# HGRN self scores by a GpSimd product and a ones matrix, with wider low-weight splits

## The chip, the cores and the metric

One core of a Trainium2 chip runs the whole program. The metric is device time in microseconds (us). Engine names follow the profile: PE is TensorE's matmul, PEld its weight load, DVE is VectorE, ACT is ScalarE, POOL is GpSimd, SP starts the DMAs.

## What is computed

A trunk of four layers over 256 tokens of 1024 features. Each layer is a half-weighted SwiGLU feed-forward block, a mixer, and a second feed-forward block, each on an RMS-normalised input and added to x. The mixers are HGRN2, neighbourhood attention, MLA, HGRN2; only the two HGRN2 layers are touched here. Cut to what matters, each of their 8 heads (128 features) does, in both directions of time:

```python
b = cumsum(logf within a chunk)
attn[t, s] = sum_d q[t, d] * exp(b[t, d] - b[s, d]) * k[s, d]      # s <= t forward, s >= t backward
o = attn @ v  (+ the state carried over from the other chunks)
```

For s = t the decay is one, so the score of a token with itself is the plain dot product of q with the sum of the forward key and the backward key, over 128 features.

## The kernel before, in words

**Layout.** Activations lie feature-major: 128 features on the partitions, 256 tokens along the row. Weights stream from HBM in slabs of 128x1024 floats, each holding eight 128x128 blocks. Products run in a split form: a weight or an activation in float32 is taken as a high part rounded to the fast format float32r and a low part, the remainder, and a product is three float32r matmuls (high by high, low by high, high by low: L352 to L354, or L399 to L401 where the activations are the stationary side).

**Slabs.** `fetch` allots a raw, a high and a low tile. `load_slab` (L330) issues the DMA, then `split` makes the high part on ACT in two copies of 512 columns (L326) and the low part on DVE by a subtraction (L327). With `long_split["on"]` the low part is one DVE instruction of 1024 columns; otherwise two of 512. The flag is on in the inner part of the feed-forward blocks (L622) and off in the mixers. `take` (L339) hands out blocks and keeps five slabs ahead.

**Order.** PE and SP run in the order in which the program is written. On ACT, DVE and POOL a planner in the framework orders the instructions by priority and by its own view of when they are ready. Every projection matmul group calls `step()`; every eighth step in HGRN calls `tick()`, which advances each pending task (a Python generator) by one `yield`, at a raised priority.

**HGRN.** `HG_ORDER` projects z and q of each head (zq0 to zq7), the gates (g0, g1) and the values (v0, v1). After each zq the generator `scores(h, ...)` is queued. Its first piece forms the decay f on ACT, the keys kq and the query q. Its second forms ks, the sum of both keys, on POOL (L723), and scales q by f on DVE (L743, L744). Then follow seven pieces for B = 1, 2, 4, ..., 64. Each piece makes four PE records of cross scores (L752), updates the queries and keys in place on DVE (L755, L757), copies the next keys on ACT (L727, the tile kc that the next piece's matmuls load), multiplies neighbouring decays on POOL (L761, tile T), and lays the scores into the tile A through a mask on DVE (L741). In the piece for B = 8 the self scores are also made: a float32 matmul of ks by q for each half of the tokens (L768), whose diagonal alone is kept by a masked copy. `outputs` then multiplies A by the values (L789) and normalises; `out_project` follows.

The tag "sq" has three buffers of 128x256; it serves squares, and the two halves `acc_r` of `row_norm`, which sums over the features by a matmul with the constant matrix of ones `ones_r` (L495).

Of the kernel before, what the change touches and what calls it, by code (L numbers as in the profile page):

```python
# [2 lines left out]
P = 128  # L3
T = 256
# [215 lines left out]
def emit(tc, i, o, plan):  # L220
# [5 lines left out]
    F32, F32R = mybir.dt.float32, mybir.dt.float32r  # L226
    I32, U8 = mybir.dt.int32, mybir.dt.uint8
    AF, ALU, AX = mybir.ActivationFunctionType, mybir.AluOpType, mybir.AxisListType
    nc = tc.nc
    V, A, G, TE = nc.vector, nc.scalar, nc.gpsimd, nc.tensor  # L230
    with ExitStack() as es:
# [10 lines left out]
        def bank(tag, shape, name):  # L242
            return pp.tile(shape, F32, tag=tag, name=name, bufs={"p": 4, "a": 3, "s": 1}[tag])

        def work(tag, shape, name, bufs=2, dt=F32):
            return wk.tile(shape, dt, tag=tag, name=name, bufs=bufs)

        def ap(t, off, dims):
            return bass.AP(tensor=t.tensor, offset=t.offset + off, ap=[list(t.ap[0])] + [list(d) for d in dims])

        def turns(t, n=T):

            return ap(t, 0, [[1, n // 2], [n // 2, 2]])

        def back(ps):

            return ap(ps, 0, [[1, 2], [2, T // 2]])

        def split2(t):
            return t.rearrange("p (a b) -> p a b", a=2)  # L260
# [6 lines left out]
        def tick():  # L267
            with tc.high_priority(URGENT):
                for g in list(tasks):
                    try:  # L270
                        next(g)
                    except StopIteration:
                        tasks.remove(g)
# [38 lines left out]
        long_split = {"on": False}  # L312
# [105 lines left out]
        ones_r = cp.tile([P, P], F32R, name="ones_r")  # L418
# [268 lines left out]
        def hgrn(s, idx, layer):  # L687
# [15 lines left out]
            def scores(h, pz, pq):  # L703
                while "R" not in nf:
                    yield
                R = nf["R"]
                z = work("w2", [P, 2, T], "z", 3)
                if len(pz) == 1:
                    V.tensor_tensor(z.rearrange("p e (a b) -> p e a b", a=2), ap(pz[0], 0, [[T, 2], [1, 2], [2, P]]), split2(R).unsqueeze(1).broadcast_to([P, 2, 2, P]), op=ALU.mult)
                else:  # L710
                    for e in range(2):
                        V.tensor_tensor(split2(z[:, e, :]), back(pz[e]), split2(R), op=ALU.mult)
                A.activation(z, z, AF.Tanh, scale=0.5)
                f = work("f", [P, 2, T], "f", 3)
                A.activation(f, z, AF.Identity, scale=c1[:, h:h + 1], bias=c0[:, h:h + 1])

                kq = work("kq", [P, 4, T], "kq", KQ_BUFS)
                A.activation(kq[:, 0::3, :], z, AF.Identity, scale=nc1[:, h:h + 1], bias=c1[:, h:h + 1])
                q = work("w1", [P, T], "q", 3)
                V.scalar_tensor_tensor(split2(q), back(pq), HG_SCALE, split2(R), op0=ALU.mult, op1=ALU.mult)  # L720
                yield
                ks = work("w1a", [P, T], "ks", 3)
                G.tensor_tensor(ks, kq[:, 0, :], kq[:, 3, :], op=ALU.add)  # L723

                def keys(B):
                    kc = work("kc", [P, T], "kc", 4)
                    A.copy(ap(kc, 0, [[2 * B, P // B], [B, 2], [1, B]]), ap(kq, 0, [[2 * B, P // B], [3 * T + B, 2], [1, B]]))  # L727
                    return kc

                def place(ps, B):  # L730
                    if B == 128:
                        A.copy(At[h][:, 1:3, :], ps)
                    elif B >= 32:
                        for a0 in range(0, P, 2 * B):
                            for sa, ta in ((a0, a0 + B), (a0 + B, a0)):
                                A.copy(At[h][sa:sa + B, 0::3, ta:ta + B], ps[sa:sa + B, :, ta:ta + B])
                    elif B == 1:
                        A.copy(At[h][:, 0::3, :], ps)
                    else:
                        m = 1 + MASK_LEVELS.index(B) if B else 0  # L740
                        V.copy_predicated(At[h][:, 0::3, :], msk[:, m:m + 1, :].broadcast_to([P, 2, P]), ps)  # L741

                V.tensor_tensor(kq[:, 2, :], q, f[:, 0, :], op=ALU.mult)  # L743
                V.tensor_tensor(kq[:, 1, :], q, f[:, 1, :], op=ALU.mult)  # L744
                kc = keys(1)
                yield
                Tt, nseg, B = f, T, 1
                while B <= 64:
                    pl = bank("a", [P, 2, P], f"A_{B}")
                    for t in range(2):  # L750
                        rhs = ap(kq, T + t * P, [[2 * B, 64 // B], [T + B, 2], [1, B]])
                        TE.matmul(pl[:, t, :], lhsT=kc[:, t * P:(t + 1) * P], rhs=rhs, start=True, stop=True)  # L752
                    n2 = nseg // 2
                    ev = ap(kq, 0, [[T, 2], [2 * B, n2], [1, B]])
                    V.tensor_tensor(ev, ev, ap(Tt, 1, [[nseg, 2], [2, n2], [0, B]]), op=ALU.mult)  # L755
                    od = ap(kq, 2 * T + B, [[T, 2], [2 * B, n2], [1, B]])
                    V.tensor_tensor(od, od, ap(Tt, 0, [[nseg, 2], [2, n2], [0, B]]), op=ALU.mult)  # L757
                    if B < 64:
                        kc = keys(2 * B)
                        Tn = work(f"T{B}", [P, 2, n2], f"T{B}", 3)  # L760
                        G.tensor_tensor(Tn, Tt[:, :, 0::2], Tt[:, :, 1::2], op=ALU.mult)  # L761
                        Tt = Tn
                    place(pl, B)
                    if B == 8:
                        pl = bank("s", [P, 2, P], "A_0")
                        for t in range(2):
                            c = slice(t * P, (t + 1) * P)
                            TE.matmul(pl[:, t, :], lhsT=ks[:, c], rhs=q[:, c], start=True, stop=True)  # L768
                        place(pl, 0)
                    nseg = n2  # L770
                    B *= 2
                    yield
                pl = bank("a", [P, 2, P], "A_128")
                TE.matmul(pl[:, 0, :], lhsT=kq[:, 3, P:], rhs=kq[:, 1, :P], start=True, stop=True)
                TE.matmul(pl[:, 1, :], lhsT=kq[:, 0, :P], rhs=kq[:, 2, P:], start=True, stop=True)
                place(pl, 128)
                scoring.discard(h)
# [43 lines left out]
            for kind in HG_ORDER:  # L821
                n = int(kind[-1])
                if kind[0] == "z":
                    if n:
                        pz = [bank("p", [P, 2, T], "z")]
                        project(pz[0][:, 0, :], xs)
                        project(pz[0][:, 1, :], xs)
                    else:
                        pz = [bank("p", [P, T], "z") for _ in range(2)]
                        beside(pz, xs)  # L830
                    pq = bank("p", [P, T], "q")
                    project(pq, xs)
                    while len(tasks) > HG_DEPTH:
                        tick()
                    scoring.add(n)
                    tasks.append(scores(n, pz, pq))
                    continue
                ps = [bank("p", [P, 512], kind) for _ in range(2)]
                natural(ps, xs, 512)
                if "h" not in nf:  # L840
                    nf["h"] = work("rh", [P, 2], "rh", 1)
                    V.tensor_scalar(nf["h"], nf["c"], 0.5, None, op0=ALU.mult)
                for t in range(2):
                    if kind[0] == "v":
                        A.activation(vt[t][n], ps[t], AF.Copy, scale=nf["c"][:, t:t + 1])
                    else:
                        half = nf["h"][:, t:t + 1]
                        gs = work("w2", [P, 512], "gs", 3)
                        A.activation(gs, ps[t], AF.Tanh, scale=half)
                        V.scalar_tensor_tensor(gt[t][n], gs, 1.0, ps[t], op0=ALU.add, op1=ALU.mult)  # L850
                if kind[0] == "g":
                    gated.append(n)
                if kind[0] == "v":
                    tasks.append(outputs(n))
            beat["every"] = 0
            tick()
            later(HG_LAST_1, tick)
            later(HG_LAST_2, tick)
# [442 lines left out]
```

## Time and profile before

| | |
|---|---|
| median of 3 runs (lowest to highest) | 1994.96 us (1994.09 to 1995.13) |
| the profiled execution's own time | 1996.11 us |
| its span, first to last instruction | 1993.8 us |
| PE busy, share of the span | 1974.6 us, 99% |
| DVE / ACT / POOL busy | 1690.8 / 1322.7 / 205.4 us |

The span is 2.3 us shorter than the profiled execution's own time, and that execution is 1.15 us slower than the median. Busy shares are averages over stages; the two HGRN stages run from about 182 to 332 us and from about 1645 to 1797 us of the span. The matmul ends in the profile are modelled: one 256-column matmul shows as 275 ns, but they overlap, so a run of them is read by the spacing of the starts, or from the chain of waits, which counts no time twice.

### The profile page before, as it was taken

How to read it: one execution, taken by the hardware profiler on the slowest of the kernel's cores; microseconds unless marked ns; L12 is line 12 of the kernel's file. 1: busy time of each engine (PE TensorE's matmuls, PEld its weight loads, DVE VectorE, ACT ScalarE, POOL GpSimd, SP SyncE). 2: the span in 40 equal slices, each digit the busy share in tenths (PEclk: the TensorE clock that was granted, in tenths of full speed). 3: DMA queues.
4: the chain of work that ended last, by engine and by line, in shares of the span. 5: the costliest groups of instructions: out<-in, count | busy, mean ns of one | idle time of the engine just before them, and what ended most of it. 6: DMA issues, size and time to landing. Idle time of an engine off the chain costs nothing.

```text
span 1993.8 us, 36877 instructions
## 1 busy us (share of the span) xinstructions
PE 1974.6 (99%) x13304; PEld 1838.4 (92%) x13304; DVE 1690.8 (85%) x3342; ACT 1322.7 (66%) x2988; POOL 205.4 (10%) x366
## 2 busy tenths in 40 slices
PE   9999999999999999999999999999999999999999
PEld 8999999999999998999999998899999999999998
DVE  8988998988888779988788879898888879989885
ACT  7665777666666578666566657676666657776663
POOL 1001320100000044100000022010000002411000
PEclk9999999999999999999999999999999999999999
DMA  6766434666666654566566653266656664445654
GB/s 229 241 203 204 149 129 136 198 209 201 199 202 202 204 203 152 170 203 203 197 201 200 202 192 128 92 196 208 201 195 204 203 210 157 141 137 177 205 169 159
DMA packets 103286, 369.34 MB, mean 185 GB/s; under 512 B 11456, under 2 KB 13248, under 8 KB 103104
## 3 DMA queue, kind: packets, MB, share of 16 engines
q1 hardware_dynamic: 103104, 366.99, 56.4%
q8 instruction: 105, 1.72, 0.4%
q14 instruction: 77, 0.63, 0.1%
HBM read 365.89 MB, written 1.05 MB: 184 GB/s over the span
## 4 chain that ended last, share of the span: by engine, by line
PE 89%; DVE 6%; ACT 2%; DMA 1%; issue 1%; POOL 0%; SPq 0%; DVEq 0%; ACTq 0%; POOLq 0%
PE gu L372 29%; PE gu L370 15%; PE dn L372 14%; PE dn L370 7%; PE A L752 2%; DVE wl L327 2%; PE out L352 1%; PE v L399 1%; PE out L354 1%; PE out L353 1%; PE v L401 1%; PE v L400 1%; PE z L352 1%; PE z L353 1%; PE z L354 1%; PE dn L354 1%
## 5 line engine op out<-in xcount | busy, mean ns | idle before, releaser
L327 DVE TENSOR_TENSOR wl<-raw,wh 128x512 fp32r<-128x512 f32 (+2 forms) x1077 | 890.8, 847 | 198.8 <-ACT wh L326 193.2
L326 ACT CAST wh<-raw 128x512 fp32r<-128x512 f32 (+1 forms) x1373 | 797.4, 617 | 362.1 <-issue 166.9
L372 PE MATMUL gu<-xw,wh 128*128 128x512 f32 x2816 | 893.6, 382 | 2.7 <-DVE xw L1249 2.5
L370 PE MATMUL gu<-xw,wl 128*128 128x256 f32 x2816 | 691.7, 273 | 0.7 <-DVE wl L327 0.7
L372 PEld LDWEIGHTS gu<-xw,wh 128*128 128x128 f32 x2816 | 504.5, 190 | 57.1 <-DVE xw L1249 3.1
L370 PEld LDWEIGHTS gu<-xw,wl 128*128 128x128 f32 x2816 | 531.2, 191 | 21.5 <-DVE wl L327 1.3
L372 PE MATMUL dn<-h,wh 128*128 128x512 f32 x1232 | 401.6, 382 | 0.0
L370 PE MATMUL dn<-h,wl 128*128 128x256 f32 x1232 | 326.9, 273 | 0.0
L372 PEld LDWEIGHTS dn<-h,wh 128*128 128x128 f32 x1232 | 229.4, 189 | 29.4
L370 PEld LDWEIGHTS dn<-h,wl 128*128 128x128 f32 x1232 | 236.2, 192 | 3.1 <-DVE wl L327 0.2
L608 ACT COPY gu<-gu 128x256 f32<-128x256 f32 x352 | 128.1, 370 | 123.5 <-PE gu L372 122.8
L609 DVE TENSOR_TENSOR gu<-gu 128x256 f32<-128x256 f32 x352 | 140.2, 417 | 5.3 <-ACT gu L608 5.3
L452 POOL TENSOR_TENSOR acc<-sq 128x256 f32<-128x256 f32 x13 | 10.6, 812 | 1121.4 <-ACT sq L449 1121.4
L399 PE MATMUL v<-wh,xw 128*128 128x256 f32 (+1 forms) x256 | 80.0, 313 | 0.0
L600 DVE SCALAR_TENSOR_TENSOR th<-th,gu 128x512 f32<-128x512 f32 (+1 forms) x96 | 61.7, 644 | 18.8 <-ACT th L599 18.8
L401 PE MATMUL v<-wh,xw 128*128 128x256 f32 (+1 forms) x256 | 77.1, 301 | 0.0
L400 PE MATMUL v<-wl,xw 128*128 128x256 f32 (+1 forms) x256 | 77.0, 301 | 0.0
L452 POOL TENSOR_TENSOR acc<-acc,sq 128x256 f32<-128x256 f32 x63 | 50.7, 804 | 248.9 <-ACT sq L449 192.0
L352 PE MATMUL out<-o,wh 128*128 128x256 f32 x256 | 73.2, 286 | 0.0
L352 PE MATMUL z<-xw,wh 128*128 128x256 f32 x256 | 73.0, 285 | 0.0
L515 ACT CAST h<-gu 128x256 fp32r<-128x256 f32 x176 | 63.3, 403 | 10.9 <-DVE gu L601 10.7
L354 PE MATMUL out<-o,wl 128*128 128x256 f32 x256 | 70.4, 275 | 0.0
(261 smaller groups left out, 3168.9 us busy)
## 6 DMA issues: line engine op xcount, KB each, us to landing
raw<-w SPq DMA_DIRECT2D x682, 512.0 KB, 4.0
bias<-bias SPq DMA_DIRECT2D x8, 512.0 KB, 4.7
raw<-w SPq DMA_DIRECT2D x7, 256.0 KB, 5.5
y<-px SPq DMA_DIRECT2D x8, 128.0 KB, 1.7
px<-x SPq DMA_DIRECT2D x3, 256.0 KB, 5.3
mskf<-c_mask SPq DMA_DIRECT2D x2, 384.0 KB, 3.9
raw<-w SPq DMA_DIRECT2D x2, 128.0 KB, 2.6
px<-x SPq DMA_DIRECT2D x1, 132.0 KB, 2.8
```

Source lines behind the costliest of these rows:

```text
L326: A.copy(h[:, b:min(b + 512, c.stop)], r[:, b:min(b + 512, c.stop)])
L327: return eng.tensor_tensor(l[:, c], r[:, c], h[:, c], op=ALU.subtract)
L352: TE.matmul(ps, lhsT=wh, rhs=turns(xh), start=first, stop=False)
L354: TE.matmul(ps, lhsT=wl, rhs=turns(xh), start=False, stop=last)
L370: TE.matmul(ps[:, 0, :], lhsT=wl, rhs=turns(xs[k][:, 0, :]), start=False, stop=stop)
L372: TE.matmul(ps, lhsT=wh, rhs=both(xs[k]), start=k == 0, stop=stop)
L399: TE.matmul(ps[t], lhsT=xh[:, c], rhs=wh, start=k == 0, stop=False)
L400: TE.matmul(ps[t], lhsT=xh[:, c], rhs=wl, start=False, stop=False)
L401: TE.matmul(ps[t], lhsT=xl[:, c], rhs=wh, start=False, stop=k == n - 1)
L515: A.copy(h, src)
L608: A.copy(split2(dst), back(ps[:, 1, :]))
L609: V.tensor_tensor(split2(dst), back(ps[:, 0, :]), split2(dst), op=ALU.add)
```

## The change

The product ks * q is made elementwise on POOL, into ks. At B = 4 it is split into a high float32r part (ACT) and a low one (POOL), in two tiles of the tag "sq". At B = 16, instead of at B = 8, two matmuls with the stationary matrix of ones sum both parts over the features into every row of a 128x256 bank, whose diagonal the same masked copy keeps, read with a stride of two. Apart from that, `long_split` is on from g0, the fourth step of HG_ORDER, to the last projection, so the 31 slabs fetched meanwhile in each HGRN stage (15 takes of zq3 to zq7, 16 of v and g) get their low part in one instruction.

```diff
@@ scores
                 kc = keys(1)
+
+                G.tensor_tensor(ks, ks, q, op=ALU.mult)
                 yield
@@ the loop over B
-                    if B == 8:
-                        pl = bank("s", [P, 2, P], "A_0")
-                        for t in range(2):
-                            c = slice(t * P, (t + 1) * P)
-                            TE.matmul(pl[:, t, :], lhsT=ks[:, c], rhs=q[:, c], start=True, stop=True)
-                        place(pl, 0)
+                    if B == 4:
+                        hl = [work("sq", [P, T], "self_r", 3, F32R) for _ in range(2)]
+                        A.copy(hl[0], ks)
+                        G.tensor_tensor(hl[1], ks, hl[0], op=ALU.subtract)
+                    if B == 16:
+                        pl = bank("s", [P, T], "A_0")
+                        for e in range(2):
+                            TE.matmul(pl, lhsT=ones_r, rhs=turns(hl[e]), start=e == 0, stop=e == 1)
+                        place(ap(pl, 0, [[1, 2], [2, P]]), 0)
@@ hgrn, over HG_ORDER
                     tasks.append(scores(n, pz, pq))
                     continue
+                long_split["on"] = True
                 ps = [bank("p", [P, 512], kind) for _ in range(2)]
@@ after the loop
             beat["every"] = 0
+            long_split["on"] = False
             tick()
```

## Rows read from the trace of the kernel before

**Rows 1.** The page's busy time by engine, and the chain that ended last.

```profile
PE 1974.6 (99%) x13304; PEld 1838.4 (92%) x13304; DVE 1690.8 (85%) x3342; ACT 1322.7 (66%) x2988; POOL 205.4 (10%) x366
...
PE 89%; DVE 6%; ACT 2%; DMA 1%; issue 1%; POOL 0%; SPq 0%; DVEq 0%; ACTq 0%; POOLq 0%
```

**Rows 2.** Busy time by stretch: window and its length, then each engine's busy us.

```profile
182.00:210.00 28.00, 27.83 (x246) 27.64 (x245) 26.82 (x56) 19.31 (x36) 8.43 (x15) 1.00 0.54 172
210.00:230.00 20.00, 20.00 (x130) 18.55 (x129) 19.98 (x46) 14.34 (x35) 6.37 (x7) 1.00 0.38 132
...
270.00:290.00 20.00, 19.63 (x149) 18.56 (x147) 19.66 (x47) 14.09 (x36) 7.25 (x14) 1.00 0.37 126
290.00:310.00 20.00, 20.00 (x132) 18.71 (x133) 16.15 (x40) 15.94 (x48) 0.00 (x0) 1.00 0.40 133
...
1580.00:1738.00 158.00, 157.83 (x1188) 151.57 (x1188) 143.01 (x309) 107.76 (x232) 35.93 (x52) 1.00 0.53 174
```

**Rows 3.** The instructions of L768 and L495: record counts, ns min/median/max, first and last start.

```profile
L768 PE MATMUL A<-q,ks x64: 275/275/275, 209.3 to 1770.0; 128*128 128x128 f32 x64
...
L495 PE MATMUL ps_R<-acc_r,ones_r x20: 272/275/275, 26.2 to 1829.6; 128*128 128x256 f32 x20
```

**Rows 4.** The chain of waits, 180 to 340 us: start us, us, what.

```profile
187.09 0.22 PE ps_R L495 x2
...
203.16 0.72 DVE wl L327
203.88 0.90 DVE kq L755
204.79 0.39 DVE kq L757
205.20 0.41 ACT kc L727
205.66 0.71 PE A L752 x4
...
209.50 0.45 PE A L768 x4
...
213.19 1.01 PE A L752 x8
216.78 1.12 PE A L752 x8
...
272.45 2.38 DVE wl L327 x3
```

**Rows 5.** PE's and its weight loader's waits for kc, whole span: us, times, longest.

```profile
PE A L752 <- ACT kc L727: 0.7, 3, 0.4
...
PEld A L752 <- ACT kc L727: 1.6, 5, 0.6
```

**Rows 6.** Groups by line and shape on POOL and ACT, 180 to 332 us.

```profile
L723 POOL TENSOR_TENSOR ks<-kq 128x256 f32<-128x256 f32 x8 | 7.7, 964 | 0.0
...
L515 ACT CAST acc_r<-acc 128x256 fp32r<-128x256 f32 x1 | 0.4, 401 | 0.0
```

**Rows 7.** The timeline, POOL and DVE together, 196 to 205 us.

```profile
196.83 0.83 DVE L744 TENSOR_TENSOR kq<-q,f 128x256 f32<-128x256 f32 x1
...
203.30 1.19 POOL L723 TENSOR_TENSOR ks<-kq 128x256 f32<-128x256 f32 x1
203.81 0.98 DVE L755 TENSOR_TENSOR kq<-kq,T 128x256 f32<-128x256 f32 x1
```

**Rows 8.** By line, whole span, ns min/median/max: L755, L741, L712 (DVE), L761 (POOL).

```profile
L755 DVE TENSOR_TENSOR kq<-kq,T x96: 403/420/979, 203.8 to 1782.9; 128x256 f32<-128x256 f32 x96
...
L741 DVE COPY_PREDICATED A<-mask,A x80: 416/441/548, 205.1 to 1777.1; 128x256 f32<-128x256 uint8 x80
...
L712 DVE TENSOR_TENSOR z<-z,R x4: 413/419/424, 194.2 to 1657.3; 128x256 f32<-128x256 f32 x4
...
L761 POOL TENSOR_TENSOR T<-T x80: 203/427/3737, 197.5 to 1752.6; 128x128 f32<-128x128 f32 x16, 128x64 f32<-128x64 f32 x16, 128x32 f32<-128x32 f32 x16, 128x16 f32<-128x16 f32 x16
```

**Rows 9.** DVE's low-weight splits by shape: 1024 columns (40 to 160 us), 512 (180 to 332).

```profile
L327 DVE TENSOR_TENSOR wl<-raw,wh 128x1024 fp32r<-128x1024 f32 x30 | 36.4, 1219 | 4.0 <-ACT wh L326 4.0
...
L327 DVE TENSOR_TENSOR wl<-raw,wh 128x512 fp32r<-128x512 f32 x82 | 54.9, 704 | 4.2 <-ACT wh L326 4.0
```

**Rows 10.** The timeline, runs of two splits: 512 columns, then 1024.

```profile
208.19 1.28 DVE L327 TENSOR_TENSOR wl<-raw,wh 128x512 fp32r<-128x512 f32 x2
...
51.11 2.35 DVE L327 TENSOR_TENSOR wl<-raw,wh 128x1024 fp32r<-128x1024 f32 x2
```

**Rows 11.** Everyone who waited for L327, whole span: us, times.

```profile
  PEld gu L370: 1.3, 2
  PE gu L370: 0.7, 1
  PEld dn L370: 0.2, 1
```

## The prediction

> **What bounds the kernel now.** First the page's busy times and the chain that ended last: PE is busy for 99% of the span and makes 89% of the chain [rows 1]. A change of PE's work therefore moves the end, one of another engine only where PE waits for it. Next the stretches of the HGRN stages: PE is busy in all but 0.17 us of 182 to 210 us and 0.37 us of 270 to 290 us, and in the second stage in all but 0.17 us [rows 2]. So both stages together have 0.7 us of PE idle time. But DVE, at 19.98 of 20 us and 19.66 of 20 us, is nearly as full as PE while the heads are scored, and falls to 16.15 us when the values come [rows 2]. The chain shows what that means: just before 205.66 us it runs through a low-weight split, two updates of kq and a copy of kc before PE goes on [rows 4]. PE's waits for kc are 0.7 us over three times, those of its weight loader 1.6 us over five [rows 5]. In the scoring part DVE is a close second bound, without slack at a few ticks.
>
> **The self-score matmuls.** Removed: L768 has 64 records, four per head (two stages of eight heads), and a head's four take 0.45 us of the chain, 0.112 us each [rows 3, 4]. Added: two float32r matmuls per head of the very form of L495, same stationary ones, 256 columns in the same order. L495 has 20 records for ten row norms, so one record per matmul, and its two take 0.22 us of the chain [rows 3, 4]. The engine thus does per head two records fewer: 2 x 0.112 x 16 = 3.6 us, all on PE, which has no slack to hide it. That is the main term: **-3.6 us**.
>
> **The work added to other engines.** Per head POOL gets a product and a subtraction of 128x256. No row shows a subtraction there with a float32r result; the nearest is L723 at 0.96 us [rows 6], so 1.9 us per head or 15 us per stage, and POOL, busy for 6 to 7 of 20 us there, has the room [rows 2]. Cost alone: nothing. ACT gets one copy like that of L515, 0.40 us [rows 6], 3.2 us per stage, on an engine busy for 14 to 16 us of 20 [rows 2]. Its price is bounded by nothing below and, where it lands just ahead of a kc copy that PE awaits, 0.4 us each time, 6.4 us over 16 heads above; I take 0, since the planner can place it anywhere in two ticks, and keep a part for the range.
>
> **The moved step.** The matmul goes from B = 8 to B = 16, one tick later, and PE, which keeps the program's order, now waits there for POOL's subtraction; behind it stand all projections. From the ACT copy at B = 4 to that matmul lie two ticks; neighbouring ticks stand 3.6 us apart in the chain (213.19 and 216.78 us) [rows 4]. The copy and the subtraction need 0.4 + 1.0 us, and the product is made three ticks earlier, so about 7 us cover 1.4 us. That cover goes only if POOL stalls: a decay product of at most 128 columns took 3.74 us at worst against a median of 0.43 us [rows 8], and even then 4.7 us fit. I take 0. The masked copy moves with it and now reads with a stride of two from PSUM. L741 itself shows 441 ns without a stride; L712, which reads PSUM with that stride, shows 419 ns, as L755 does from SBUF [rows 8]. Between no change and one more median (0.44 us, 7 us of DVE over 16 heads) I take no change. Of the three buffers of "sq" a pair is held for two ticks; heads start 24 steps, three ticks, apart, so pairs don't meet, and the squares of `outputs` use the third. No DMA is added or moved; SP waits at no new place.
>
> **The wide low weights.** Two splits of 512 columns back to back take 1.28 us, two of 1024 take 2.35 us, so 1.18 us for a slab [rows 10]: 0.10 us saved. By the means it is 2 x 704 - 1219 = 189 ns [rows 9]. For 31 slabs that is 3.1 to 5.9 us of DVE time per stage; I take the lower, since the splits mostly run in pairs. On PE's path it is worth nothing directly: in the whole span only L370, in the feed-forward blocks, waited for L327, never a projection of HGRN [rows 11]. It can only help as relief for the kq and kc chain. Against that, an urgent update can stand behind a split for 1.2 us where it was 0.7 us [rows 9].
>
> **What POOL does to DVE.** While L723 ran on POOL, an update L755 took 0.98 us against a median of 0.42 us, and L744 took 0.83 us beside a POOL product that size [rows 7, 8]. The 0.98 us one is the 0.90 us piece of the chain before PE's wait at 205.66 us [rows 4]. A new POOL operation thus costs DVE between 0 and 0.56 us; the median of all 96 updates, 0.42 us, beside a minimum of 0.40 us, says that most are hardly touched, so I take 0.2 us: 16 new ones per stage make 3.2 us, which the 3.1 us of the wide splits pay back. Net on DVE: nothing; on PE's waits: nothing, within about 1 us either way.
>
> The Trainium skill, GPSIMD Engine Reference, section "Engine selection", sends an elementwise product to VectorE and not to GpSimd, and its "Key points" name the contention with DVE instructions that have two SBUF inputs. By that rule alone, with every new POOL operation on the path, the sum would turn from a gain to a loss; rows 7 agree that the contention is there, and whether it reaches PE is the third rival below.
>
> **The sum.** The profiled execution's own time is 1996.11 us (its span 1993.8 us); less 3.6 us this is 1992.5 us. It was 1.15 us above the median, so against the median: 1994.96 - 3.6 = **1991.4 us**. A measurement of this kernel tells about 0.2% from no change, 4.0 us: faster means below 1991.0 us, slower above 1998.9 us. The forecast falls just inside "the same".
>
> **Rivals.**
> - *Relief.* The wide splits free DVE earlier and PE's waits shrink as well. For it: the chain runs through runs of two and three splits (2.38 us at 272.45 us) [rows 4]. Against it: POOL's share. The 0.7 us of idle time gives 1990.7 us; with the waits of PE and its weight loader on kc all gone (0.7 + 1.6 us, which partly count the same time) 1989.1 us. That is faster by over 0.2%; the planner orders DVE, ACT and POOL anew, which can also turn out so. Chance 0.36.
> - *Half given back.* The ACT copies or the subtraction come late at a few ticks: five kc copies behind a 0.4 us copy make 2.0 us, so 1993.4 us; eight of 32 POOL operations at 0.5 us on a chain without slack make 4.0 us, so 1995.4 us. Still the same. Chance 0.16.
> - *DVE becomes the bound.* The place is the update of kq ahead of the kc copy, the price 0.56 us for each POOL operation that meets one on a chain without slack. It decides from 14 of 32 on (14 x 0.56 = 7.8 us, less 3.6 us); with all 32 it is 17.9 - 3.6 = 14.3 us, so 2009.3 us. For it: DVE's 98 to 100% [rows 2]. Against it: PE's waits for kc number 3 and 5 in 112 pieces of B up to 64 [rows 5], and most POOL operations run now without making any. Chance 0.08.
> - *It does not do what it says*: if the ones matmuls took two passes like the float32 ones, nothing would be saved, 1995 us. L495's one record per matmul [rows 3] leaves no room for it; chance 0, and it would be the same anyway.
>
> **How the numbers follow.** The forecast as summed, 1991.0 to 1993 us, has 0.40; it counts as the same, with the half given back 0.56. Relief makes 0.36 faster, the DVE bound 0.08 slower. The range goes from all waits gone, 1989.1 us, to eight stretched updates, 1995.4 us; the forecast's own is 1991.0 to 1993 us.
>
> **What would show it.** Right: 32 records of the ones matmul for 64 of L768, 0.22 us per head in the chain; DVE splits of 1024 columns in the HGRN stages; PE's waits for kc near 0.7 and 1.6 us; no wait of PE on the POOL subtraction. Wrong: a new PE wait for POOL or ACT at the ones matmul, L755 and L757 with medians well above 0.42 us and more PE waits for kc, the squares of `outputs` waiting for a buffer, or a feed-forward or attention stage whose length changed, which none of these steps explains.

## The result, and the profile after

The changed kernel takes 2024.16 us in the median (2021.41 to 2026.71, 4 runs) against 1995.05 us, a ratio of 1.0143, 95% interval 1.0131 to 1.0156. The profiled execution took 2025.16 us, with a span of 2023.4 us: 29.6 us more than before, where 3.6 us less were forecast.

The page of the changed kernel, busy time by engine and the chain that ended last:

```profile
PE 1982.5 (98%) x13272; PEld 1842.6 (91%) x13272; DVE 1693.6 (84%) x3280; ACT 1327.1 (66%) x3004; POOL 227.8 (11%) x398
...
PE 85%; DVE 7%; ACT 3%; POOL 2%; issue 2%; DMA 1%; SPq 0%; POOLq 0%; DVEq 0%; ACTq 0%
```

Against [rows 1] PE has 32 records fewer, as forecast, but PE, idle for 1993.8 - 1974.6 = 19.2 us of the span before, is idle for 2023.4 - 1982.5 = 40.9 us now, and POOL, which had 0% of the chain, has 2% of it. The stretches say where; columns as in [rows 2], the clock being the third number from the end:

```profile
182.00:210.00 28.00, 25.49 (x211) 25.30 (x210) 21.66 (x47) 16.15 (x31) 8.73 (x17) 0.94 0.42 137
210.00:230.00 20.00, 19.16 (x120) 17.34 (x119) 19.82 (x40) 14.88 (x36) 7.71 (x9) 1.00 0.48 159
...
250.00:270.00 20.00, 17.48 (x139) 17.29 (x137) 12.60 (x24) 12.73 (x27) 6.61 (x11) 0.91 0.36 119
270.00:290.00 20.00, 18.25 (x159) 17.87 (x157) 20.00 (x41) 12.08 (x30) 12.66 (x13) 1.00 0.35 119
290.00:310.00 20.00, 18.45 (x112) 17.30 (x113) 16.63 (x35) 15.33 (x40) 9.27 (x12) 0.91 0.31 107
...
1720.00:1740.00 20.00, 15.23 (x111) 14.85 (x110) 10.52 (x19) 10.81 (x26) 8.50 (x13) 0.88 0.33 113
```

The loss lies in the two HGRN stages, in which nearly every stretch shows PE idle by 1 to 5 us. DVE is now far from full in some of them (12.60 and 10.52 of 20 us), where it was nearly full before:

```profile
250.00:270.00 20.00, 20.00 (x178) 20.00 (x177) 18.70 (x44) 14.89 (x33) 6.31 (x12) 1.00 0.42 138
...
1720.00:1740.00 20.00, 20.00 (x177) 20.00 (x176) 20.00 (x48) 14.51 (x35) 11.11 (x12) 1.00 0.39 132
```

So DVE isn't the bound there; something ahead of it is late. What is late stands in the waits. PE's and ACT's waits by line (us, times, longest), then the idle time of POOL before L769, the new subtraction:

```profile
PE A L754 <- ACT kc L727: 22.3, 15, 2.5
...
ACT self_r L768 <- POOL ks L747: 32.2, 12, 4.4
...
  PE A L773: 40.2, 4
```

PE's wait for kc, 0.7 us over three times before [rows 5], is 22.3 us. ACT waits in L768, the copy of the high part, for POOL's product L747. And POOL waits for PE's ones matmul L773 over the three buffers. Two suspects, then. The timeline of the first stall, POOL, ACT, DVE and PE together, shows the first at work:

```profile
198.22 0.53 ACT L727 COPY kc<-kq 128x256 f32<-128x256 f32 x1
...
200.27 0.73 POOL L747 TENSOR_TENSOR ks<-ks,q 128x256 f32<-128x256 f32 x1
...
201.03 0.41 ACT L768 CAST self_r<-ks 128x256 fp32r<-128x256 f32 x1 [2.28 <-POOL ks L747]
201.34 0.62 ACT L713 ACTIVATE z<-z 128x512 f32<-128x512 f32 x1
201.87 0.60 ACT L326 CAST wh<-raw 128x512 fp32r<-128x512 f32 x1
...
202.51 0.69 DVE L327 TENSOR_TENSOR wl<-raw,wh 128x512 fp32r<-128x512 f32 x1 [3.05 <-ACT wh L326]
203.11 0.42 DVE L720 SCALAR_TENSOR_TENSOR q<-q,R 128x256 f32<-128x256 f32 x1
...
204.09 0.62 DVE L759 TENSOR_TENSOR kq<-kq,f 128x256 f32<-128x256 f32 x1
...
204.73 0.44 ACT L727 COPY kc<-kq 128x256 f32<-128x256 f32 x1
205.22 0.75 PE L754 MATMUL A<-kq,kc 128*128 128x128 f32 x4 [2.51 <-ACT kc L727]
```

The program has L768 in the piece for B = 4, behind the kc copies for B = 2, 4 and 8. The planner put it on ACT right behind the kc copy for B = 1, ahead of all three. ACT runs nothing of what stands behind L768 and stands still for 2.28 us until POOL has made the product; DVE then waits 3.05 us for a weight copy that stands behind L768, its updates of kq come late, and the kc copy for B = 2 with them. PE waits 2.51 us. In the chain of a later stall the same link closes directly, POOL's queue, the copy, the kc copy, PE:

```profile
257.48 0.68 POOL ks L723
258.16 0.18 POOL T L763
...
258.61 0.69 POOL ks L747
...
259.33 0.03 ACT self_r L768
...
259.64 0.43 ACT kc L727
...
260.12 0.89 PE A L754 x4
261.01 0.21 PE z L352
```

The last row is a second loss: z matmuls that took 0.11 us each take 0.21 us. The stretch 206 to 209 us, right behind the first stall, shows it too, with a granted clock of half:

```profile
206.00:209.00 3.00, 3.00 (x16) 3.00 (x16) 1.25 (x2) 1.55 (x4) 1.57 (x4) 0.50 0.00 1
...
core 0: 2023.4 us, clock 0.995
```

That is 1.2 for 2.4 GHz. The mean clock of 0.995 over 2023.4 us means 10.1 us of full-speed work not done, against 2.0 us at the 0.999 before. The Trainium skill, TensorE: Matmul & The Clock Gate, section "What's actually happening", says that the array's clock is gated to half when it has been idle; the trace agrees on the level, at 0.50 behind a stall of 2.51 us.

The sum: 21.7 us more idle time, 8.1 us more lost to the clock, 3.6 us of work saved make 26.2 of the 29.6 us. Read in windows of 1 us, the granted clock falls at six places of the two HGRN stages and costs 10.3 us there, and at none of them before, which would make the sum 28.4 us. The rest isn't assigned: the mean clock has three digits, and short waits hide under the modelled ends of matmuls.

### The profile page after: what moved, and what is told of

Same layout as the page of the kernel before. It is cut to its first block, busy times and chain, and to the rows that moved or that the text cites. A ratio compares the mean times of both kernels' runs of the same rounds, so it can differ in the third digit from the quotient of the medians.

```text
span 2023.4 us, 36807 instructions
## 1 busy us (share of the span) xinstructions
PE 1982.5 (98%) x13272; PEld 1842.6 (91%) x13272; DVE 1693.6 (84%) x3280; ACT 1327.1 (66%) x3004; POOL 227.8 (11%) x398
## 4 chain that ended last, share of the span: by engine, by line
PE 85%; DVE 7%; ACT 3%; POOL 2%; issue 2%; DMA 1%; SPq 0%; POOLq 0%; DVEq 0%; ACTq 0%
PE gu L372 29%; PE gu L370 15%; PE dn L372 13%; PE dn L370 7%; DVE wl L327 2%; PE A L754 2%; PE out L352 1%; PE out L354 1%; PE v L399 1%; PE out L353 1%; PE v L401 1%; PE v L400 1%; POOL T L763 1%; PE dn L354 1%; PE dn L352 1%
## 5 line engine op out<-in xcount | busy, mean ns | idle before, releaser
L327 DVE TENSOR_TENSOR wl<-raw,wh 128x512 fp32r<-128x512 f32 (+2 forms) x1015 | 885.6, 889 | 208.4 <-ACT wh L326 203.3
L754 PE MATMUL A<-kq,kc 128*128 128x128 f32 x448 | 71.2, 294 | 22.6 <-ACT kc L727 22.3
L754 PEld LDWEIGHTS A<-kq,kc 128*128 128x128 f32 x448 | 60.7, 195 | 28.1 <-ACT kc L727 27.3
L352 PE MATMUL z<-xw,wh 128*128 128x256 f32 x256 | 76.5, 299 | 0.0
L353 PE MATMUL z<-xw,wh 128*128 128x256 f32 x256 | 73.9, 289 | 0.0
```

The costliest lines, as they stand in the source:

```text
L327: return eng.tensor_tensor(l[:, c], r[:, c], h[:, c], op=ALU.subtract)
L352: TE.matmul(ps, lhsT=wh, rhs=turns(xh), start=first, stop=False)
L353: TE.matmul(ps, lhsT=wh, rhs=turns(xl), start=False, stop=False)
```

## The experiments

Theory A: the early copy on ACT. Theory B: the three buffers. Theory C: the wide splits. Each time is a median; each ratio is to the kernel before, run on the same chip.

**Taking the change apart.** `self_only` leaves out the line that turns `long_split` on, so that the splits stay narrow; `wide_only` has nothing but the two `long_split` lines.

> The self-score change alone, the wide low-weight splits off. Theory A (on ACT the planner put the high-part copy of the product, L768, ahead of the kc copy for B = 2; it waits for POOL's product, 32.2 us in 12 waits, and the kc copies wait behind it in order): 2018 to 2028 us, PE's waits for kc again about 22 us. Theory B (POOL's subtraction waits 40.2 us for PE's matmul of an earlier head, for want of a fourth buffer, and the decay products wait behind it): the same 2018 to 2028 us. Theory C (the wide splits hold DVE for 1.2 us ahead of the updates of kq): 1990 to 2000 us.

> The wide low-weight splits alone, self scores as before. Theories A and B: 1993 to 1997 us, no measurable difference, since nobody in HGRN waits for a low weight; PE's waits for kc stay at about 0.7 us. Theory C: 2010 us or more.

Measured: self_only 2022.95 us, ratio 1.0146 (1.0131 to 1.0161); wide_only 1992.81 us, ratio 0.9992 (0.9984 to 1.0001). self_only has the whole loss, and PE's waits for kc are 22.4 us in it: the loss belongs to the self scores, and C falls.

**The copy, or the buffers.** `copy_behind_keys` and `own_buffers` each change one thing in the changed kernel, `both` has the two:

```diff
+                    last_kc[0] = A.copy(...)        # the kc copy in keys()
-                        A.copy(hl[0], ks)
+                        with tc.issue_after(last_kc[0].ins):
+                            A.copy(hl[0], ks)
...
-                        hl = [work("sq", [P, T], "self_r", 3, F32R) for _ in range(2)]
+                        hl = [work("oh", [P, T], "self_r", 8, F32R) for _ in range(2)]
```

> The changed kernel with the high-part copy tied on ACT behind the kc copy of the same piece (B = 4), where the program has it; buffers and wide splits as in the changed kernel. Theory A: PE's waits for kc fall below 3 us and the time to 1989 to 1996 us. Theory B: POOL's waits for PE at the subtraction stay and the time stays at 2010 us or more. Theory C: 2010 us or more.

> The changed kernel with the two parts in the tag of oh (eight buffers, idle while the heads are scored) instead of sq (three); ACT's order as the planner makes it. Theory A: ACT's waits for the product stay at about 30 us and the time at 2015 to 2028 us, while POOL's waits for PE go to 0. Theory B: 1989 to 2000 us. Theory C: 2010 us or more.

Measured: copy_behind_keys 1998.34 us, ratio 1.002 (1.0011 to 1.0029); own_buffers 2031.08 us, ratio 1.0188 (1.0172 to 1.0203). The idle time before L768 in own_buffers, then PE's wait for kc in copy_behind_keys:

```profile
  POOL ks L747: 42.3, 16
```

```profile
PE A L756 <- ACT kc L729: 4.4, 9, 0.7
```

Moving one copy in ACT's order takes about 25 us of the 29 away (3.7 us above the kernel before are left), and the clock is back (mean 1.000). With buffers to spare POOL waits for PE no more, but ACT's copy waits for POOL at every one of the 16 heads instead of 12, and the kernel is slower still. B falls. A holds in the main, with two misses: copy_behind_keys came 2 us above the 1989 to 1996 us expected, with 4.4 us of PE's waits for kc where less than 3 us were expected, and own_buffers 3 us above its 2015 to 2028 us.

> The changed kernel with the high-part copy tied on ACT behind the kc copy of its piece, and the two parts in the eight buffers of oh. If the 3.7 us that copy_behind_keys stands above the kernel before come from the buffers: 1989 to 1993 us. If they come from POOL's subtraction, which stands in POOL's order ahead of the next head's decay products and waits there for ACT's copy: still 1996 to 2000 us, with POOL's waits for the copy at 60 us or more.

Measured: 1999.01 us, ratio 1.0021 (1.0012 to 1.003). What is left doesn't come from the buffers. POOL's subtraction waits 103.7 us for ACT's copy here, as the second expectation has it; pool_own, below, has no such wait and is no faster, so that wait isn't it either.

**Is the copy enough?** `pool_one` and `act_early` leave the float32 self scores as they were. pool_one adds POOL's product, which nobody reads, and act_early adds to that the copy, also unread:

```diff
                 kc = keys(1)
+                extra = work("oh", [P, T], "extra", 8)
+                G.tensor_tensor(extra, ks, q, op=ALU.mult)
                 yield
...
+                    if B == 4:                                   # act_early alone
+                        more = work("oh", [P, T], "more", 8, F32R)
+                        A.copy(more, extra)
```

> pool_one (the kernel before with POOL's product, unread) with one more thing: the float32r copy of that product on ACT, unread too, which the planner again puts ahead of the kc copy for B = 2. Theory A: that copy is enough, 2015 to 2035 us, ACT's waits for the product at 30 us or more and PE's for kc at 20 us or more. If the new matmuls or the shared buffers are needed for the loss: 1999 to 2005 us.

Measured: 2028.15 us, ratio 1.0162 (1.0148 to 1.0176), where pool_one has 1.0017. ACT's and PE's waits in act_early:

```profile
ACT more L768 <- POOL extra L747: 41.5, 16, 4.3
```

```profile
PE A L754 <- ACT kc L727: 25.5, 16, 3.2
```

A dead copy of 0.40 us, 16 times, adds 29 us, as much as the whole loss, without the matmuls, the three buffers or the wide splits.

**The copy on POOL.** `copy_on_pool` has `G.tensor_copy(hl[0], ks)` for `A.copy(hl[0], ks)` in the changed kernel, so ACT has no part in it; `pool_own` adds the eight buffers.

> The changed kernel with the high-part copy on POOL instead of ACT, so that no ACT instruction waits for POOL; three buffers as in the change. Theory A (ACT's early copy holds the kc copies): no ACT wait for ks, PE's waits for kc below 5 us, 1989 to 1998 us; what is left above 1991.5 us are POOL's waits for PE over the three buffers. Theory B (buffers alone): POOL's waits for PE stay at 30 us or more and the time at 2010 us or more.

> As copy_on_pool, and the two parts in the tag of oh (eight buffers). Theory A with the term of the forecast (two PE records fewer per head, 3.6 us): no wait of POOL for PE, PE's waits for kc at or below 1 us, 1989 to 1993 us. If the POOL operations stretch DVE's updates on the path (rival of the prediction): PE's waits for kc of 4 us or more and 1995 us or more.

Measured: copy_on_pool 2001.71 us, ratio 1.0038 (1.0025 to 1.0051); pool_own 2000.4 us, ratio 1.003 (1.0019 to 1.004), with 6.4 us of PE's waits for kc. Again most of the loss is gone with the ACT wait, and again 6 to 8 us above the kernel before are left, 9 to 10 us above the forecast. Both came above the range of theory A. In copy_on_pool POOL still waits 40.9 us for PE over the three buffers, in pool_own not at all, and the intervals overlap: those waits cost little or nothing. pool_own meets its second expectation, POOL operations that stretch DVE's.

**What is left: POOL's load.** `pool_load` has pool_one's product and a subtraction on POOL (`G.tensor_tensor(more, ks, extra, op=ALU.subtract)` at B = 4), the results unread.

> The kernel before (float32 self scores, narrow splits) with two more POOL operations of 128x256 per head, a product and a subtraction whose results nobody reads: the price of POOL's load on DVE alone. If contention is small: 1994 to 1998 us and L755's median at 0.42 us. If 0.56 us of each of the 32 reached PE: 2012 us.

> The kernel before with one more POOL operation per head (the product alone, its result unread), for two in pool_load. If each POOL operation costs about the same: 1997 to 2001 us, half of pool_load's 10 us. If a threshold decides (DVE full from a certain load on): 1994 to 1996 us.

Measured: pool_load 2004.45 us, ratio 1.0047 (1.0034 to 1.0059); pool_one 1999.17 us, ratio 1.0017 (1.0008 to 1.0026). The two operations cost about 9 us, between the two expectations for pool_load; the product alone costs about 3 us, a third, within the 1997 to 2001 us expected if each operation costs about the same. The page of pool_load, and DVE's groups of 182 to 338 us, first three of before, then three of pool_load, then PE's wait for kc in pool_load:

```profile
PE 1976.5 (99%) x13304; PEld 1837.7 (92%) x13304; DVE 1703.2 (85%) x3342; ACT 1322.6 (66%) x2988; POOL 232.6 (12%) x398
```

```profile
L327 DVE TENSOR_TENSOR wl<-raw,wh 128x512 fp32r<-128x512 f32 x81 | 54.3, 704 | 4.0 <-ACT wh L326 3.8
...
L755 DVE TENSOR_TENSOR kq<-kq,f 128x256 f32<-128x256 f32 x8 | 4.6, 570 | 0.0
...
L744 DVE TENSOR_TENSOR kq<-q,f 128x256 f32<-128x256 f32 x8 | 4.3, 540 | 0.0
```

```profile
L327 DVE TENSOR_TENSOR wl<-raw,wh 128x512 fp32r<-128x512 f32 x81 | 57.0, 733 | 4.0 <-ACT wh L326 3.8
...
L744 DVE TENSOR_TENSOR kq<-q,f 128x256 f32<-128x256 f32 x8 | 5.3, 664 | 0.0
L757 DVE TENSOR_TENSOR kq<-kq,f 128x256 f32<-128x256 f32 x8 | 5.1, 639 | 0.0
```

```profile
PE A L754 <- ACT kc L727: 5.5, 13, 0.7
```

The split's mean went from 704 to 733 ns, that of L744 from 540 to 664 ns, that of the first update of kq (L755, here L757) from 570 to 639 ns, and PE waits for kc 13 times instead of 3 [rows 5]. Over the whole span DVE's 3342 instructions, the same number as before [rows 1], take 1703.2 us for 1690.8 us: 12.4 us, or 0.39 us for each new POOL operation. A rival is that POOL's longer queue makes its decay products T late; the trace speaks against it, as no engine is shown waiting for a T of POOL in pool_load. `on_vector` takes the new work off POOL: copy_behind_keys with `V` for `G` in the product and the subtraction.

> copy_behind_keys with the product and the subtraction on DVE instead of POOL: no new POOL operation at all. If the 3.7 us that copy_behind_keys stands above the kernel before come from POOL operations stretching DVE's: DVE now pays 32 x about 0.37 us itself, 12 us over both stages, so PE's waits for kc stay at 3 us or more and the time at 1995 to 2003 us. If they come from POOL's order (the subtraction stands there ahead of decay products): 1989 to 1993 us.

Measured: 2001.67 us, ratio 1.0032 (1.002 to 1.0044), PE's waits for kc 7.2 us. With no new POOL operation the loss is about the same, as expected of a full DVE that pays for the work itself. It isn't a clean test, though: the product on DVE now waits for the sum of the keys that POOL makes, 9.2 us over nine times, 4.4 us of it from 182 to 338 us, the same kind of wait that ACT had:

```profile
L749 DVE TENSOR_TENSOR ks<-ks,q 128x256 f32<-128x256 f32 x8 | 3.4, 422 | 4.4 <-POOL ks L723 4.4
```

The rule of the Trainium skill weighed in the prediction, VectorE for an elementwise product (GPSIMD Engine Reference, "Engine selection"), gains nothing here: 1.0032 on DVE against 1.002 on POOL, intervals overlapping; what it would gain without that wait no run shows.

`pool_late` and `pool_late_apart` put the same two POOL operations into `outputs`, behind the copy of oh, with results in the tag "sq" or in the otherwise idle "w1b":

```diff
                     os_.append(oh)
+                    extra = work("w1b", [P, 2, P], "extra")
+                    G.tensor_tensor(extra, oh, oh, op=ALU.mult)
+                    more = work("w1b", [P, 2, P], "more", dt=F32R)
+                    G.tensor_tensor(more, oh, extra, op=ALU.subtract)
```

> The kernel before with two more POOL operations of 128x256 per head, as many as in pool_load, but in outputs, where the values come and DVE is busy for 32.2 of 42 us; their results are unread. If the price needs a full DVE: 1994 to 1997 us, both HGRN stages within 1 us of the kernel before. If POOL's load costs wherever it is: 2000 us or more.

> pool_late with the unread results in two buffers that nothing else uses in that stretch, so that no other engine waits for POOL. If POOL's price needs a full DVE: a ratio of 0.999 to 1.001, both HGRN stages within 0.5 us of the kernel before. If its load costs wherever it is: 1.002 or more.

Measured: pool_late 2000.96 us, ratio 1.0024 (1.0015 to 1.0033), in the range expected if the load costs wherever it is, but through "sq" ACT's squares waited 6.6 us for POOL, so it doesn't tell the load from the buffers; pool_late_apart 1998.82 us, ratio 1.0018 (1.0009 to 1.0027), between its two expectations. DVE was busy for 32.20 of 42 us there, 77%, in the kernel before:

```profile
290.00:332.00 42.00, 41.99 (x263) 38.84 (x264) 32.20 (x86) 32.41 (x103) 0.00 (x0) 1.00 0.39 131
```

The price is under half of pool_load's: higher where DVE is full, and not nothing where it is not. How it reaches PE there stays open; PE's waits for kc, 2.0 us for 0.7 us, are only a part.

**The wide splits.** `behind_narrow` is copy_behind_keys without the line that turns `long_split` on; `wide_again` repeats wide_only; `wide_everywhere` lets `load_slab` split 1024 columns at a time in every stage of the kernel before.

> copy_behind_keys with the wide splits off. If the wide splits are relief for DVE in this kernel too, as in wide_only: 1999 to 2003 us, 1 to 4 us above copy_behind_keys. If they are a burden (1.2 us ahead of an update): below 1998 us.

> wide_only once more, the same kernel. If its 1.6 us were a gain: a ratio below 1 whose interval leaves out 1, both HGRN stages shorter by 0.5 to 1 us. If not: a ratio of 0.999 to 1.001 about 1.

> The kernel before with the low part made 1024 columns at a time in all stages. If wide splits free DVE time where DVE is close to PE (HGRN, the attention mixers): 1989 to 1994 us. If they only help in HGRN: 1992 to 1995 us as wide_only; if a late first half of a slab holds PE at a stage's start: 1995 us or more, with PE waits for wl.

Measured: behind_narrow 2000.89 us, ratio 1.0027 (1.0017 to 1.0038), beside 1.002 for copy_behind_keys; wide_again 1994.41 us, ratio 0.9994 (0.9986 to 1.0003); wide_everywhere 2002.82 us, ratio 1.0036 (1.0022 to 1.0049). In HGRN the wide splits point to a gain of 1 us or so in three comparisons, none clear of noise, and PE's waits for kc point the same way (7.6 us in behind_narrow, 4.4 us in copy_behind_keys). Made wide in every stage they cost 7 us; as wide_only and wide_again lose nothing, that must lie mainly outside the stretch that the change widens, and its cause stays open. No version tried beats the kernel before by more than its noise; wide_only comes nearest.

## Why the prediction was wrong

- **The main term** held as far as the trace shows it: 32 fewer records, and the ones matmuls take 0.22 us per head in the chain, as [rows 4] have it for L495. That they give 3.6 us back isn't measured by itself. It fits that behind_narrow, with POOL operations as many as pool_load's and the new matmuls, has 1.0027 where pool_load has 1.0047, though the intervals just overlap.

```profile
217.82 0.22 PE A L773 x2
```

- **The step that failed** is the price of the ACT copy: "I take 0, since the planner can place it anywhere in two ticks", with 6.4 us as the upper bound. The bound counted the copy's own 0.40 us and not its wait: while the copy waited for POOL's product, nothing behind it on ACT ran. That was 32.2 us over 12 waits on ACT, and PE's waits for kc came to 22.3 us, against 4.4 us in copy_behind_keys. The section on the moved step looked for a wait on PE and found 7 us of cover for it, and there it was right: PE never waited for the subtraction. The cover was counted from where the program has the copy; at the first stall the planner put it three kc copies earlier, where nothing covers it. None of the rivals has this: *Half given back* has a copy that lies just ahead of a kc copy, but prices it at 0.4 us, and the 0.08 for slower stood on another mechanism.
- **The clock** wasn't in the sum at all. In the HGRN stages before, where PE's stalls for kc were at most 0.4 us [rows 5], the granted clock was 1.00 in every stretch of [rows 2]; in the changed kernel it fell to half behind six of the seven stalls of 2.2 to 2.5 us. The loss isn't a fixed price of a stall: in act_early, with 25.5 us of such waits, it fell at two places, for 3.4 us.
- **The buffers**: "pairs don't meet" was wrong. POOL waited 40.2 us for PE over them. It cost nothing that own_buffers, both or pool_own could give back.
- **POOL on DVE**: the mechanism was right, the size off. "Net on DVE: nothing" came out as about 9 us for 32 operations (pool_load), 0.29 us each at the end of the run, against 0.2 us each on DVE, set off against the wide splits. The third rival had the place right; its 0.56 us for each operation on a chain without slack is above what was measured. It isn't what made the 29 us: with the ACT wait gone (copy_behind_keys) what is left is 4 us. That fits the parts: the 9 us of pool_load, less 3.6 us of the main term and 1 us or so of the wide splits. The 98 to 100% that it rests on are the fullest of five stretches; over 182 to 290 us DVE was busy for 96%.
- **The wide splits**, worth nothing directly: right, 0.9992 and 0.9994.

## What to carry to other kernels

When a planner orders an engine, price a new instruction there by what it waits for, times all that stands behind it, and not by its own length: a 0.4 us copy that reads another engine's fresh result may be put at the first place where the planner holds it ready, and if the producer is later on the chip, the whole queue stands. Tie such an instruction behind one whose inputs come later; here that one line took away about 25 of 29 us. Work for an idle engine isn't free either when a nearly full neighbour runs slower beside it (DVE's same instructions took 12.4 us longer in pool_load): measure it first as a dead operation.

## What the runs showed that was not expected

- Stalls of PE of 2.2 to 2.5 us mostly cost more than themselves: the granted clock was 0.50 in 206 to 209 us, and over the run 8.1 us more than before went that way by the mean clock.
- Two unread POOL operations of 128x256 per head, on an engine busy for 10% of the span, cost 9 us (1.0047), in a stretch where they came beside DVE at 96%; two more of that size cost 4 us (1.0018) beside a DVE at 77%.
- Giving the changed kernel the buffers that it waits for made it slower, a ratio of 1.0188 for 1.0143: ACT now waits for POOL's product at all 16 heads, 42.3 us for 32.2 us.
